# Cross attention's first half: heads 0 to 2 in an order written by hand, with the first two query products between the last output tiles

## The chip, the cores and the metric

The kernel runs on one core of a Trainium2 chip. The metric is the device time of one execution in microseconds (us); lower is better. The names of the engines are those of the profile: PE is TensorE's matrix multiply and PEld its weight load, DVE is VectorE, ACT is ScalarE, POOL is GpSimd, and SP is the engine whose queue issues the DMAs.

## What is computed

The reference is one decoder layer on 1024 tokens of width 1024, in float32. Only the middle of it is touched: the output product of the mixer adds to x, x is normalized by rows, and four cross-attention heads of width 256 read 256 memory tokens.

```python
x = x + jnp.concatenate([ml_out, fx_out], axis=-1) @ w_out[l]
x = x + cross_attention(rmsnorm(x, ln_x[l]), rmsnorm(mem, ln_mem[l]), w_xq[l], w_xkv[l], w_xo[l])
...
def cross_attention(h, memn, w_q, w_kv, w_o):
    q = (h @ w_q).reshape(B, S, X_HEADS, X_DH)
    ...
    s = jnp.einsum('bqhd,bmhd->bhqm', q, k) * (X_DH ** -0.5)
    p = jax.nn.softmax(s, axis=-1)
    o = jnp.einsum('bhqm,bmhd->bqhd', p, v).reshape(B, S, D)
    return o @ w_o
```

## The kernel before

Activations lie with features on the 128 partitions and tokens along the free axis. Every float32 product is made of three matmuls: each operand is cut into a rounded part (`hi`, copied by ACT, line 134 or 137) and the rest (`lo`, subtracted by DVE, line 135 or 138), and `mm3` (lines 186 to 188) adds lo by hi, hi by lo and hi by hi. The weight's lo part comes first, so a product can't start before DVE has cut its weights.

The tokens are worked in two halves of 512 (`hf` 0 and 1). The stage around the change runs so:

- Output tiles. There are 16 of them, 8 row blocks `n` in each half: nine matmuls of 128x512 each, in the order hf 0 with n 0 to 3, hf 1 with n 0 to 3, then the same with n 4 to 7. `full_sink` adds the residual that was loaded from `x1d` (DVE, line 1126), stores the sum, cuts it into `h2` for the first half (lines 137 and 138), and sums squares into `x1_accs[hf]`: the square is ACT's (line 222), the addition POOL's (line 226).
- `row_second(hf)` turns those sums into 1/rms. Four products with a column of ones (PE, line 234), then `rsqrt_cols`: DVE line 198, POOL line 204 (a power), DVE lines 206 to 208, which write `rcol`. For the second half `to_row` follows: PE transposes `rcol` (line 249), ACT copies it (line 250), and SP stores it to `rowd` and loads it back, spread over the partitions, as `row` (lines 251 and 253).
- The first half of each head `hd`. `query_whole` makes the two query products (24 matmuls of 128x512 each, into the banks `mm` and `m2`; the listings and the trace write `m` for `m2`) and cuts each into hi and lo. `right_side(hd)` prepares the second half's operands: two loads from `x1d`, a scaling by ACT (line 1177), seven cuts and four subtractions by POOL (line 1339), of which one feeds the next. `cross_head` loads the head's keys and values (lines 1276 and 1277), makes 24 score matmuls of 128x256, takes row maxima (DVE, lines 1289 and 1291), exponentials (ACT, line 1293), reciprocals (DVE, line 1294), scales the probabilities (ACT, line 1296), transposes them on PE (line 1301), and makes the two value products (12 matmuls of 128x512) into the single bank `ov`.
- The second half's heads follow, by blocks, with queries made in `query_blocks` from operands that `left_query` prepares.

Nothing in this stage has a fixed order before the change: the scheduler places each engine's instructions by its own model of time, subject to their dependencies. `in_order` is a helper that the first and the last stage use. Within it every compute engine (PE, ACT, DVE, POOL) keeps the order in which the code is written; SP's queue is still placed by the scheduler. Once compiled, either kernel has one fixed list of instructions for each engine, and an instruction that waits holds up all that stand behind it on its engine.

## Time and profile before

| what | value |
|---|---|
| median of the three runs | 1512.61 us |
| lowest and highest run | 1509.36 and 1513.43 us |
| profiled execution: span from first to last instruction, the only time that the page gives for it | 1509.2 us |
| PE busy | 1493.0 us, 99% of the span |
| PE weight loads busy | 1263.7 us, 84% |
| DVE / ACT / POOL busy | 1122.7 / 757.7 / 528.7 us |
| stage at hand: last output tiles, first half of the heads | about 592 to 705 us |

Times in the profile count from the span's start. A timeline row gives the start, the duration, the engine, the line, the operation and its output and inputs, and in brackets the idle time ahead of it with what ended it. Matmuls are pipelined: a 128x512 matmul is shown with about 0.39 us, but the next one starts 0.23 us after it. PEclk is the share of full clock that TensorE was granted.

### The profile page before, as it was taken

The numbers are of one execution on the slowest core, as the hardware profiler recorded it, in microseconds if no ns is written. First come the engines' busy times: TensorE is split into PE (matmuls) and PEld (weight loads), VectorE is DVE, ScalarE is ACT, GpSimd is POOL, SyncE is SP. The second block draws the span as 40 slices with busy tenths as digits, with TensorE's granted clock in tenths as the row PEclk, the third lists the DMA queues.
The fourth block names the chain that finished last, engine by engine and source line by source line (L and its number), as shares of the span: only waits on it lengthen the run. The fifth ranks groups of instructions, "written<-read, shape, count | busy, mean of one in ns | idle before, by whom it ended". The sixth has DMA issues, their size and how long they took to land.

```text
span 1509.2 us, 22358 instructions
## 1 busy us (share of the span) xinstructions
PE 1493.0 (99%) x7806; PEld 1263.7 (84%) x7806; DVE 1122.7 (74%) x1803; ACT 757.7 (50%) x1440; POOL 528.7 (35%) x545
## 2 busy tenths in 40 slices
PE   9999999999999999999999999999999999999997
PEld 9988888889899888788988878888888888888887
DVE  7766676664788875667767899989996678787765
ACT  7324343334688764566654467566664521122134
POOL 1003030414365441623300044454544365553312
PEclk9999999999999999999999999999999999999999
DMA  6322333435777877853354447676678677776623
GB/s 243 115 79 95 98 108 126 132 129 153 247 261 256 284 248 246 271 169 126 128 182 159 147 155 279 235 261 248 217 273 292 264 279 279 279 272 251 247 88 112
DMA packets 124276, 303.04 MB, mean 201 GB/s; under 512 B 13810, under 2 KB 28460, under 8 KB 117252
## 3 DMA queue, kind: packets, MB, share of 16 engines
q1 hardware_dynamic: 124164, 301.62, 57.3%
q8 instruction: 61, 1.00, 0.3%
q14 instruction: 51, 0.42, 0.1%
HBM read 202.75 MB, written 98.82 MB: 200 GB/s over the span
## 4 chain that ended last, share of the span: by engine, by line
PE 90%; DMA 4%; DVE 3%; ACT 1%; issue 1%; POOL 1%; POOLq 0%; DVEq 0%; SPq 0%; ACTq 0%
PE tp L186 8%; PE tp L187 8%; PE tp L188 8%; PE sc L186 6%; PE sc L188 6%; PE sc L187 6%; PE mm L186 5%; PE m L188 5%; PE m L186 5%; PE m L187 5%; PE mm L188 5%; PE mm L187 5%; PE ov L801 2%; PE ov L186 2%; PE ov L187 2%; PE ov L188 2%
## 5 line engine op out<-in xcount | busy, mean ns | idle before, releaser
L186 PE MATMUL tp<-act,wl 128*128 128x512 f32 (+1 forms) x440 | 172.6, 392 | 0.0
L187 PE MATMUL tp<-act,wh 128*128 128x512 f32 (+1 forms) x440 | 172.1, 391 | 0.0
L188 PE MATMUL tp<-act,wh 128*128 128x512 f32 (+1 forms) x440 | 171.8, 392 | 0.0
L135 DVE TENSOR_TENSOR wl<-wr,wh 128x1024 fp32r<-128x1024 f32 (+2 forms) x99 | 131.4, 1327 | 27.0 <-ACT wh L134 26.7
L134 ACT ACTIVATE wh<-wr 128x1024 fp32r<-128x1024 f32 (+2 forms) x99 | 99.8, 1008 | 85.7 <-PE tp L188 32.7
L186 PE MATMUL mm<-act,wl 128*128 128x512 f32 (+1 forms) x332 | 124.8, 376 | 2.6 <-DVE r_c L138 2.1
L188 PE MATMUL mm<-act,wh 128*128 128x512 f32 (+1 forms) x332 | 124.1, 374 | 0.0
L187 PE MATMUL mm<-act,wh 128*128 128x512 f32 (+1 forms) x332 | 123.8, 373 | 0.0
L186 PE MATMUL m<-act,wl 128*128 128x512 f32 (+1 forms) x308 | 113.8, 369 | 0.6 <-DVE wl L135 0.6
L188 PE MATMUL m<-act,wh 128*128 128x512 f32 (+1 forms) x308 | 113.8, 369 | 0.0
L187 PE MATMUL m<-act,wh 128*128 128x512 f32 (+1 forms) x308 | 113.7, 369 | 0.0
L188 PE MATMUL sc<-act,wh 128*128 128x512 f32 (+1 forms) x280 | 105.6, 377 | 0.0
L187 PE MATMUL sc<-act,wh 128*128 128x512 f32 (+1 forms) x280 | 105.6, 377 | 0.0
L186 PE MATMUL sc<-act,wl 128*128 128x512 f32 (+1 forms) x280 | 105.6, 377 | 0.0
L1612 POOL TENSOR_TENSOR z<-wr 128x256 f32<-128x256 f32 x56 | 52.9, 966 | 131.8 <-DMA wr<-w_ff2q 126.7
L188 PEld LDWEIGHTS tp<-act,wh 128*128 128x128 f32 x440 | 82.7, 188 | 19.0
L186 PEld LDWEIGHTS tp<-act,wl 128*128 128x128 f32 x440 | 82.7, 188 | 18.5
L187 PEld LDWEIGHTS tp<-act,wh 128*128 128x128 f32 x440 | 82.7, 188 | 18.2
L134 ACT ACTIVATE wh<-z 128x1024 fp32r<-128x1024 f32 (+1 forms) x54 | 55.5, 1027 | 81.8 <-POOL z L1612 62.3
L135 DVE TENSOR_TENSOR wl<-z,wh 128x1024 fp32r<-128x1024 f32 (+1 forms) x54 | 77.7, 1439 | 11.4 <-ACT wh L134 11.4
L134 ACT ACTIVATE w<-wr 128x768 fp32r<-128x768 f32 (+3 forms) x35 | 28.0, 801 | 107.4 <-PE tp L186 33.0
L186 PEld LDWEIGHTS mm<-act,wl 128*128 128x128 f32 x332 | 62.7, 189 | 14.2 <-DVE r_c L138 2.6
(734 smaller groups left out, 4387.2 us busy)
## 6 DMA issues: line engine op xcount, KB each, us to landing
act<-right SPq DMA_DIRECT2D x49, 1024.0 KB
right<-w SPq DMA_DIRECT2D x56, 256.0 KB
wr<-w_ff2q SPq DMA_DIRECT2D x28, 512.0 KB
right<-r_d SPq DMA_DIRECT2D x49, 256.0 KB
right<-r_e SPq DMA_DIRECT2D x49, 256.0 KB
act<-fqk SPq DMA_DIRECT2D x48, 256.0 KB
wr<-w_in SPq DMA_DIRECT2D x20, 512.0 KB
wr<-w_ff SPq DMA_DIRECT2D x20, 512.0 KB
```

What stands on the lines that cost most here:

```text
L134: s.activation(hi, src, AF.Copy)
L135: return v.tensor_tensor(out=lo, in0=src, in1=hi.bitcast(F32), op=ALU.subtract)
L186: nc.tensor.matmul(ps, w[1], x[0], start=first, stop=False, skip_group_check=more)
L187: nc.tensor.matmul(ps, w[0], x[1], start=False, stop=False, skip_group_check=more)
L188: nc.tensor.matmul(ps, w[0], x[0], start=False, stop=last, skip_group_check=more)
L801: nc.tensor.matmul(self.ov[:, c0:], self.fv[:, self.j], t[:, c0:], start=self.j == 0 and t is self.p[1], stop=self.last and t is self.p[0])
L1612: g.tensor_tensor(out=o, in0=x, in1=y, op=op)
```

## The change

The 16 output tiles become a generator, of which 14 run as before. Then, inside `in_order`, come the sums of `row_second(0)`, the first query product, the tile n = 6 of hf 1, the second query product and the tile n = 7. Heads 0 to 2 follow in written order: scores, the next head's first query product, transposes, the next head's second query product, values. `row_second(1)` and `to_row` stand inside head 0. For these three heads GpSimd scales the probabilities, and the second value product goes to a `tp` bank. Head 3 and all that follows stay with the scheduler.

```diff
     def row_second(hf):
         rsqrt_sums(x1_accs[hf], rcol[:, 4 * hf : 4 * hf + 4], 4)
-        if hf:
-            to_row(row, rcol, 8, rowd[2:3])
...
+    full = full_tiles()
+    for _ in range(14):
+        next(full)
...
+    def query_weights(n):
+        if n < KT:
+            w_query[n] = weights(a["w_xq"][n])
+
+    def query_product(n):
+        if n < KT:
+            ((_, _, p_query[n]),) = proj(w_query.pop(n), [h2], 1, order=[(0, 0)], into=ps_tile(("mm", "m2")[n % 2]))
+
+    def query_cut(n):
+        if n < KT:
+            queries[n] = q_room(n % 2)
+            split(*queries[n], p_query.pop(n), 1.0 / 16.0)
...
         for i in range(4):
-            s.activation(pr[:, i], pr[:, i], AF.Copy, scale=rden[:, i : i + 1])
+            if hf == 0 and hd < XH - 1:
+                g.tensor_scalar(out=pr[:, i], in0=pr[:, i], scalar1=rden[:, i : i + 1], scalar2=1.0, op0=ALU.mult, op1=ALU.mult)
+            else:
+                s.activation(pr[:, i], pr[:, i], AF.Copy, scale=rden[:, i : i + 1])
...
-            ov = ov_()
+            ov = tp() if kk and hf == 0 else ov_()
...
+    banks[:] = ["tp"]
+    row_second(0)
+    with in_order():
+        for n in range(2):
+            query_weights(n)
+        query_product(0)
+        next(full)
+        query_cut(0)
+        query_product(1)
+        next(full)
+        query_cut(1)
+        query_weights(2)
+        for hd in range(XH - 1):
+            steps = cross_head(hd, 0, [queries.pop(2 * hd + kk) for kk in range(2)], *os_[0])
+            next(steps)
+            query_product(2 * hd + 2)
+            if hd == 0:
+                row_second(1)
+            query_weights(2 * hd + 3)
+            side = right_steps(hd)
+            next(side)
+            next(steps)
+            query_cut(2 * hd + 2)
+            query_product(2 * hd + 3)
+            if hd == 0:
+                to_row(row, rcol, 8, rowd[2:3])
+            next(side, None)
+            query_weights(2 * hd + 4)
+            query_cut(2 * hd + 3)
+            for _ in steps:
+                pass
+    banks[:] = ["mm", "tp", "m2", "tp"]
+    right_side(XH - 1)
...
```

`right_steps` is `right_side` as a generator: its first step loads and scales and makes the three plain cuts, its second makes the subtractions and the cuts of their results.

What the compiled lists of instructions make of this is shown at three places. A name ends in the buffer's number; "waits" names the engines or DMA queues whose semaphores the instruction waits for.

First place, PE between the last output tiles and the first query product. Before: `tp_7092` is the last tile (hf 1, n 7), the line 234 products sum `r_b_6786`, which is `x1_accs[0]`, and `mm_7130` is the first query.

```order
L186 MATMUL tp_7092<-w_1275_6767,wl_6949 128x512
L187 MATMUL tp_7092<-w_1275_6767,wh_6948 128x512
L188 MATMUL tp_7092<-w_1275_6767,wh_6948 128x512
L234 MATMUL ov_7079<-ones,r_b_6786 128x1 [waits PE_49,Pool_49]
L234 MATMUL ov_7079<-ones,r_b_6786 128x1 x3
L186 MATMUL mm_7130<-act_6784,wl_7127 128x512 [waits DVE_49]
```

After, at the same place; `tp_7045` is the tile n 5 of hf 1, two tiles earlier, and `mm_7100` the first query:

```order
L187 MATMUL tp_7045<-w_1275_6767,wh_6942 128x512
L188 MATMUL tp_7045<-w_1275_6767,wh_6942 128x512
L234 MATMUL ov_7075<-ones,r_b_6786 128x1 [waits PE_49,Pool_49]
L234 MATMUL ov_7075<-ones,r_b_6786 128x1 x3
L186 MATMUL mm_7100<-act_6784,wl_7091 128x512 [waits DVE_49]
```

The sums of the first half stand two output tiles earlier on PE; the tiles n 6 and n 7 now come behind the first and the second query product. SP's list is the same in both kernels up to and with the stores of the tiles n 4 and n 5 of hf 1.

Second place, ACT at the end of the output tiles. Before: `r_c_7106` is the square of the last tile, `r_b_7122` and `r_p_7157` the hi cuts of the first and second query; the others belong to `right_side(0)` and to weights.

```order
L222 ACTIVATE r_c_7106<-r_p_7102 128x512 [waits DVE_49,Pool_49]
L134 ACTIVATE act_7192<-r_f_7197 128x256 [waits Activation_49]
L134 ACTIVATE act_7194<-r_f_7197 128x256
L134 ACTIVATE act_7193<-r_f_7196 128x256 [waits Pool_49]
L134 ACTIVATE act_7194<-r_f_7196 128x256 [waits Pool_49]
L137 ACTIVATE r_b_7122<-mm_7130 128x512 [waits PE_49]
L134 ACTIVATE wh_7358<-wr_7356 128x1024 [waits DMAHW6_49]
L134 ACTIVATE act_7193<-r_f_7196 128x256 [waits Pool_49]
L137 ACTIVATE r_p_7157<-m_1357_7165 128x512 [waits DMAHW7_49,DMAHW2_49,PE_49]
```

After; `r_c_7139` and `r_c_7185` are the squares of the tiles n 6 and n 7:

```order
L222 ACTIVATE r_c_7139<-r_e_7135 128x512 [waits DVE_49,Pool_49]
L137 ACTIVATE r_b_7142<-mm_7100 128x512 [waits PE_49]
L222 ACTIVATE r_c_7185<-r_p_7181 128x512 [waits DVE_49,Pool_49]
L137 ACTIVATE r_p_7188<-m_1352_7146 128x512 [waits DMAHW4_49,DMAHW7_49,DMAHW2_49,PE_49]
L134 ACTIVATE wh_7194<-wr_7192 128x1024
```

The last tile's square now stands directly ahead of the second query's cut, and the work of `right_side(0)` behind the exponentials. On DVE the last tile's addition likewise stands directly ahead of the second query's lo cut.

Third place, `row_second(1)` and `to_row`. Before, on DVE, they stood among head 2's row maxima; `c_var`, `c_t` and the last `rcol` row are `row_second(1)`, and `wl_7787` is a weight for the second half of the tokens:

```order
L198 TENSOR_SCALAR c_var_7306<-ov_7301 128x4 [waits PE_49]
L1289 TENSOR_REDUCE c_mx_7597<-sc_7599 128x2 [waits PE_49]
L1291 TENSOR_TENSOR c_mx_7597<-c_mx_7597,rcol 128x2 [waits DVE_49]
L206 TENSOR_TENSOR c_t_7310<-c_y_7308 128x4 [waits Pool_49]
L207 SCALAR_TENSOR_TENSOR c_t_7310<-c_t_7310,c_var_7306 128x4 [waits DVE_49]
L1294 RECIPROCAL c_rden_7596<-c_den_7595 128x4 [waits Activation_49]
L208 SCALAR_TENSOR_TENSOR rcol<-c_t_7310,c_y_7308 128x4 [waits DVE_49]
L138 SCALAR_TENSOR_TENSOR r_c_7670<-mm_7677,r_b_7669 128x512 [waits Activation_49]
L135 TENSOR_TENSOR wl_7787<-wr_7770,wh_7786 128x1024 [waits PE_49,Activation_49]
```

After, on DVE, in head 0; `wl_7290` is the lo cut of the weights for the product that stands on PE directly behind the transposes:

```order
L1306 RECIPROCAL c_rden_7208<-c_den_7207 128x4 [waits Activation_49]
L198 TENSOR_SCALAR c_var_7279<-ov_7274 128x4 [waits PE_49]
L206 TENSOR_TENSOR c_t_7283<-c_y_7281 128x4 [waits Pool_49]
L207 SCALAR_TENSOR_TENSOR c_t_7283<-c_t_7283,c_var_7279 128x4 [waits DVE_49]
L208 SCALAR_TENSOR_TENSOR rcol<-c_t_7283,c_y_7281 128x4 [waits DVE_49]
L135 TENSOR_TENSOR wl_7290<-wr_7287,wh_7289 128x1024 [waits DMAHW7_49,Activation_49]
```

Before, on ACT, around the copy of `row`; only work for the second half of the tokens and a value cut follow it:

```order
L134 ACTIVATE wh_7879<-wr_7772 128x1024 [waits Pool_49]
L250 ACTIVATE row<-ov_7314 8x128 [waits PE_49]
L1253 ACTIVATE r_f_7878<-mm_7883 128x256 [waits PE_49]
L134 ACTIVATE act_7120<-ov_7476 128x512 [waits PE_49]
L134 ACTIVATE w_1494_7915<-wr_7911 128x512 [waits DMAHW4_49,DMAHW3_49,PE_49]
```

After, on ACT, in head 0; `r_b_7323` and `r_p_7373` are the hi cuts of head 1's queries, and `act_7294`, `act_7295` the cuts of `right_steps`:

```order
L137 ACTIVATE r_b_7323<-mm_7249 128x512
L250 ACTIVATE row<-ov_7352 8x128 [waits PE_49]
L134 ACTIVATE act_7294<-r_f_7297 128x256 [waits Pool_49] x2
L134 ACTIVATE act_7295<-r_f_7297 128x256 [waits Pool_49]
L134 ACTIVATE wh_7369<-wr_7367 128x1024 [waits DMAHW3_49]
L137 ACTIVATE r_p_7373<-m_1391_7327 128x512 [waits DMAHW2_49]
```

Both have moved from the end of the first half into head 0, and what stands behind them on DVE and ACT is now what head 0's and head 1's next products on PE take. On PE the line 234 products of `row_second(1)` stand behind a whole query product (head 1's first) and the transpose of `rcol` (line 249) behind the next one (head 1's second). On SP the store and the load of `row` now stand ahead of the load of head 1's keys.

## The prediction

> **What bounds the kernel now.** I read the page, then the waits of PE in the stage at hand, then the granted clock there.

> ```profile
> PE 1493.0 (99%) x7806; PEld 1263.7 (84%) x7806; DVE 1122.7 (74%) x1803; ACT 757.7 (50%) x1440; POOL 528.7 (35%) x545
> PE 90%; DMA 4%; DVE 3%; ACT 1%; issue 1%; POOL 1%; POOLq 0%; DVEq 0%; SPq 0%; ACTq 0%
> PE mm L186 <- DVE r_c L138: 2.1, 1, 2.1
> ```

> PE is busy for 99% of the span and holds 90% of the chain that ended last, so a time that PE waits is added to the span. The third line is the whole answer on PE's waits between 592 and 700 us: one wait, before the first scores. It cost more than it shows:

> ```profile
> 639.20 0.39 PE L188 MATMUL m<-act,wh 128*128 128x512 f32 x1
> 641.74 0.50 PE L186 MATMUL mm<-act,wl 128*128 128x512 f32 x1 [2.14 <-DVE r_c L138]
> 639.05:642.46 3.41, 1.27 (x6) 0.74 (x5) 3.01 (x5) 2.86 (x7) 2.18 (x3) 1.00 0.64 252
> 642.46:645.88 3.42, 3.42 (x11) 2.65 (x10) 2.59 (x4) 2.10 (x4) 0.00 (x0) 0.50 0.87 287
> 1495.80:1499.20 3.40, 2.91 (x26) 2.71 (x24) 2.61 (x6) 2.04 (x6) 1.84 (x3) 1.00 0.46 157
> 1499.20:1502.60 3.40, 1.68 (x12) 1.40 (x12) 1.13 (x6) 0.78 (x2) 0.71 (x1) 1.00 0.44 152
> 1502.60:1506.00 3.40, 0.08 (x1) 0.00 (x0) 2.48 (x4) 0.00 (x0) 0.00 (x0) 0.50 0.47 159
> ```

> The first number after a stretch is its length, the next PE's busy time, and the last but two the granted clock. The stretch in which PE was busy for 1.27 of 3.41 us was followed by one of 3.42 us at clock 0.50; 1.68 of 3.40 near the end did the same, 2.91 of 3.40 did not. At half clock 3.42 us do the work of 1.71. So the one wait cost 2.1 + 1.7 = 3.8 us. This is all that the change can win in a stage without other waits: 0.25% of 1512.6.

> [...]

> **The change part by part.** The count of matmuls stays. What matters is where PE finds its next input late. Instructions that move are counted by what stands ahead of them on their engine now.

> (a) The sums of `row_second(0)` stand behind the tile n 5 of hf 1, two tiles earlier.

> ```profile
> 616.42 0.80 SPq L1125 DMA_DIRECT2D r_d<-x1d  x2
> 621.69 0.69 DVE L1126 TENSOR_TENSOR r_d<-m,r_d 128x512 f32<-128x512 f32 x1 [2.95 <-DMA r_d<-x1d]
> 623.80 3.00 POOL L226 TENSOR_TENSOR r_b<-r_c,r_b 128x512 f32<-128x512 f32 x2 [2.56 <-ACT r_c L222]
> 622.92 0.39 PE L188 MATMUL tp<-w,wh 128*128 128x512 f32 x1
> 627.35 0.95 PE L234 MATMUL ov<-ones,r_b 128*128 128x1 f32 x8
> 628.16 0.48 PE L186 MATMUL mm<-act,wl 128*128 128x512 f32 x1
> ```

> The residual of hf 0, n 6, lands for the addition at 621.69, though it was issued at 616.42. The squares of n 6 and n 7 are therefore added by POOL until 623.80 + 3.00 = 626.80. Before, line 234 came to PE at 627.35 and found the sum ready. Now PE is there at 622.92 + 0.23 = 623.15 and waits until 626.85: **3.7 us**. SP's, ACT's, DVE's and POOL's lists up to there are unchanged, so nothing comes sooner, and on PE both query products and two tiles are queued behind. The bounds: if the load lands without its 2.95 us of waiting, the sum is done about 3 us sooner and 0.7 is left; upwards I allow 0.5 us more, since PE's way to this point is the same.

> (b) Tile n 7 now lies between the second query product and the scores, as its cover. But ACT and DVE treat tile n 7 before they cut that query. From the tile's last matmul to the scores: DVE's addition, ACT's square, ACT's hi cut, DVE's lo cut.

> ```profile
> 631.07 0.68 DVE L1126 TENSOR_TENSOR r_p<-tp,r_p 128x512 f32<-128x512 f32 x1
> 627.16 0.61 ACT L222 ACTIVATE r_c<-r_d 128x512 f32<-128x512 f32 x1
> 641.93 0.59 ACT L137 ACTIVATE r_p<-m 128x512 fp32r<-128x512 f32 x1
> 641.01 0.68 DVE L138 SCALAR_TENSOR_TENSOR r_c<-mm,r_b 128x512 fp32r<-128x512 f32 x1
> ```

> 0.68 + 0.61 + 0.59 + 0.68 = 2.56, with handovers of about 0.05 each (641.01 + 0.68 to PE's 641.74) and 0.16 of drain 2.9; less ACT's overlap of the two (0.1), and three scores of 0.12 that need only the first query: **2.4 us**. So the old 2.14 us wait is not removed, only made by another chain. Bounds 2.0 and 2.9.

> (c) Head 0. Its third query product (head 1's first, 5.6 us) covers the softmax, see (e). Behind it come line 234 for `row_second(1)`, 8 transposes, and the next product, whose lo weights DVE cuts only after `rcol`.

> ```profile
> 679.27 1.03 PE L1301 MATMUL tp<-ident,z 128*128 128x128 f32 x8
> 631.67 0.15 DVE L198 TENSOR_SCALAR c_var<-ov 128x4 f32<-128x4 f32 x1
> 686.92 1.03 POOL L204 TENSOR_TENSOR c_y<-c_var,half 128x4 f32<-128x4 f32 x1
> 687.98 1.26 DVE L206 TENSOR_TENSOR c_t<-c_y 128x4 f32<-128x4 f32 x1 [1.01 <-POOL c_y L204]
> 689.28 0.16 DVE L207 SCALAR_TENSOR_TENSOR c_t<-c_t,c_var 128x4 f32<-128x4 f32 x1
> 690.16 1.22 DVE L135 TENSOR_TENSOR wl<-wr,wh 128x1024 fp32r<-128x1024 f32 x1
> ```

> From line 234's start: 0.95 + 0.15 + 1.03 + three small steps of 0.16 to 0.2 (0.6) + 1.22 + handovers (0.16) = 4.1 us. PE has 0.81 (627.35 to 628.16) and 0.87 of transposes (the row's 1.03 less a last drain) to do: it waits **2.4 us**. Nothing makes this shorter; if line 206 takes the 1.26 that it took beside POOL's work, 3.5.

> (d) Head 1's scores wait for its second query, which ACT cuts behind the copy of `row`, which waits for the transpose of `rcol` behind that same query product. From its end: line 250, cut t1, POOL's second and third subtraction, cut t3, weights, DVE's lo weights, DVE's lo cut.

> ```profile
> 693.85 0.25 ACT L250 ACTIVATE row<-ov 8x128 f32<-8x128 f32 x1
> L134 ACT ACTIVATE act<-r_f 128x256 fp32r<-128x256 f32 x24 | 9.1, 413 | 4.8 <-POOL r_f L1339 4.6
> L135 DVE TENSOR_TENSOR act<-r_f,act 128x256 fp32r<-128x256 f32 x24 | 12.2, 528 | 10.8 <-ACT act L134 10.5
> L1339 POOL TENSOR_TENSOR r_f<-r_f,r_f 128x256 f32<-128x256 f32 x8 | 6.5, 812 | 9.2 <-DVE act L135 4.7 <-ACT r_f L1177 4.2
> L134 ACT ACTIVATE wh<-wr 128x1024 fp32r<-128x1024 f32 x15 | 15.9, 1057 | 2.3 <-DMA wr<-w_xq 1.2 <-POOL wr L1227 1.1
> 696.76 0.33 SPq L251 DMA_DIRECT2D rowd<-row  x1
> 700.30 0.32 SPq L253 DMA_DIRECT2D row<-rowd  x1
> 642.11 0.38 SPq L1276 DMA_DIRECT2D w<-kxd  x1
> 645.59 0.41 PE L186 MATMUL sc<-w,r_c 128*128 128x256 f32 x1
> ```

> 0.25 + 0.41 + 0.53 + 0.81 + 0.81 + 0.41 + 1.06 + 1.22 + 0.68 = 6.2, with handovers 6.6 us. PE has 12 value matmuls of 0.233 and three scores of 0.12: 3.15. It waits 3.4 us at least. SP may add to it: the store of `row` waits for the same copy, its load for the store (3.5 us, 696.76 to 700.30), and only then go head 1's keys, which in head 0 landed within 3.5 us (642.11 to 645.59). That would be 0.4 + 3.5 + 0.4 + 3.5 = 7.8 us after the product, a wait of 5.0. The store took its 3.5 us in a busier stretch, so I stay between: **4.2 us**.

> (e) Scaling by GpSimd, 4 x 0.53 instead of ACT's 4 x 0.51:

> ```profile
> L767 POOL TENSOR_SCALAR w<-w,c_den 128x256 f32<-128x256 f32 x8 | 4.2, 528 | 2.1 <-DVE c_den L764 1.5 <-ACT r_a L137 0.5
> L1296 ACT ACTIVATE z<-z,c_rden 128x256 f32<-128x256 f32 x16 | 6.8, 509 | 0.0
> L1293 ACT ACTIVATE z<-sc,c_mx,rcol 128x256 f32<-128x256 f32 x16 | 8.8, 559 | 4.1 <-DVE c_var L198 3.3 <-DVE c_mx L1291 0.8
> 685.71 0.68 DVE L1289 TENSOR_REDUCE c_mx<-sc 128x2 f32<-128x512 f32 x1
> ```

> After the last score: maximum and product 0.9, two exponentials 1.3, reciprocal 0.2, POOL 2.1, handovers 0.3: 4.8 us, beside a query product of 24 x 0.233 = 5.6. Covered by 0.8; if POOL took twice as long, PE would wait 1.3 in each head. The second value bank costs nothing and, as PE never waited for `ov`, saves nothing. In heads 1 and 2 the second query's cut ends some 8.3 us after the transposes, against 5.6 + 2.8 + 0.35 of PE's work: covered by under half a microsecond, so I count **0.5 us** for both, bounds 0 and 4 (head 2 has the weights of the second half among its cuts).

> Sum of waits: 3.7 + 2.4 + 2.4 + 4.2 + 0.5 = 13.2. Each of the first four is as long as the one that halved the clock, but a gap may fall across two stretches, and then neither need be idle enough: I count three falls of four, 5.1 us. Less the old 3.8: **+14.5 us**. The span was 1509.2, near the lowest run, 1509.36; on the median of 1512.6 it makes 1527.1.

> **Rivals.**
> - The written order is covered, not slower: at each place what PE needs is ready. Then only the old wait goes: 1512.6 - 3.8 = 1508.8. It decides at (d): the chain of 6.6 us must end within PE's 3.15. For it speaks that (e) fits; against it, that three chains hang on PE's own position and can't run ahead.
> - The late load of (a) was an accident of this execution and SP's part of (d) is hidden: 0.7 + 2.4 + 2.4 + 3.4 + 0.5, two clock falls of 1.7, less 3.8: +9.0, 1521.6.
> [...]
> - More waits in heads 1 and 2 and where head 3 meets the second half's operands, whose cuts stand ahead of head 2's exponentials on ACT and wait for a DMA: up to 4 more, the fourth clock fall and one more (3.4): +21.9, 1534.5.

> **How the numbers follow.** Forecast 0.42, around 1527; early load 0.20; clock only after long gaps 0.12; more waits 0.11; covered 0.08; and 0.07 for a part of the waits only, 1511 to 1516. Leaving out the last two, the range is 1516 to 1537: the lower end takes every wait at its lower bound with one clock fall (0.7 + 2.0 + 2.4 + 3.4 + 1.7 - 3.8 = +6.4, and a run 3 us under the median), the upper the last rival with 2 us for the spread of the runs (1509.36 to 1513.43). A difference within 0.3% (4.5 us) can't be told from none. Covered is within it, but for a spread in its favour (0.04 faster); of the partial case about half is the same: faster 0.04, same 0.08, slower 0.88.

> **What would show it.** Right: PE waits of line 234 for POOL's `r_b` near 623 us (3.7), of the first scores for DVE's `r_a` (2.3), of `m` line 186 for `wl` (2.4) directly behind head 0's transposes, of head 1's scores for `r_y` or the keys' DMA (3.4 to 5), each with clock 0.5 soon behind it. No wait for POOL at the transposes. Wrong: PE without waits from 623 to 700 us, or line 234 finding its sum ready.

## The result and the profile after

| what | before | after |
|---|---|---|
| median (lowest to highest), four runs each | 1511.67 us (1509.36 to 1513.43) | 1538.22 us (1536.42 to 1541.62) |
| span of the profiled execution | 1509.2 us | 1539.9 us |
| ratio after to before | | 1.018, 95% interval 1.0167 to 1.0192 |

The change costs 26.5 us. The forecast had said slower, by 14.5; 1538.2 lies 1.2 us above its range. The profiled execution is the slowest of the four (1541.62 us for a span of 1539.9), so the two spans differ by 30.7. The mean granted clock was 0.990 in it and 0.991 in the other three, which fits one or two slow stretches fewer there (an estimate from these means).

On the page, PE's busy time has grown by 10.8 us with the same 7806 matmuls, which is a slower clock (granted 0.990 in the mean, 0.997 before); the rest of the 30.7 is waiting:

```profile
PE 1503.8 (98%) x7806; PEld 1272.1 (83%) x7806; DVE 1125.2 (73%) x1803; ACT 753.7 (49%) x1428; POOL 534.8 (35%) x557
```

PE's waits between 600 and 770 us, where before there was one of 2.1 and one of 0.4:

```profile
PE sc L186 <- DMA w<-kxd: 4.2, 1, 4.2
PE sc L186 <- DVE r_y L138: 3.5, 2, 2.5
PE ov L234 <- POOL r_b L226: 3.4, 1, 3.4
PE sc L186 <- DVE r_a L138: 2.4, 1, 2.4
PE m L186 <- DVE wl L135: 2.2, 1, 2.2
PE mm L186 <- ACT r_f L1265: 2.0, 1, 2.0
PE sc L186 <- ACT act L134: 1.1, 1, 1.1
PE m L187 <- DVE act L135: 1.0, 1, 1.0
PE tp L1316 <- POOL z L1309: 0.8, 2, 0.5
PE sc L187 <- DVE act L135: 0.5, 1, 0.5
PE ov L186 <- ACT row L250: 0.4, 1, 0.4
```

The numbers are the sum, the count and the longest. Together 21.5 us. The rows with `r_b`, `r_a`, `wl`, `row` and `kxd` are the four foreseen places, 12.6 us. The transposes and head 3's scores (`r_y`, once 2.5) make 3.3. What is left, 5.6 us, lies behind head 3's scores, at the first products of the second half's queries (`r_f`, `act`) and at its first scores (`r_y`, once 1.1).

The clock, by stretches (length, PE's busy time, ..., granted clock third from the end):

```profile
625.25:628.66 3.41, 1.01 (x9) 1.01 (x10) 3.41 (x4) 2.49 (x4) 2.78 (x3) 1.00 0.69 228
628.66:632.07 3.41, 3.41 (x10) 2.67 (x10) 1.36 (x3) 0.00 (x0) 3.41 (x3) 0.50 0.98 314
673.03:676.45 3.42, 0.13 (x1) 0.00 (x0) 3.15 (x5) 2.13 (x4) 0.16 (x1) 1.00 0.98 293
676.45:679.86 3.41, 2.51 (x12) 2.54 (x13) 0.31 (x1) 0.00 (x0) 0.00 (x0) 0.50 1.02 404
679.86:683.27 3.41, 3.41 (x16) 3.31 (x16) 1.28 (x3) 1.20 (x4) 0.00 (x0) 0.50 0.83 333
717.41:720.82 3.41, 1.53 (x14) 1.33 (x12) 3.41 (x4) 1.76 (x5) 2.96 (x3) 1.00 0.63 182
720.82:724.23 3.41, 2.84 (x24) 2.84 (x25) 3.41 (x6) 3.17 (x7) 1.81 (x2) 1.00 0.32 123
```

There are five falls: near 629, 649 and 663 for one stretch each, near 676 and 731 for two each. That is 23.9 us at half clock, with PE busy for 22.0 of it, so 11.0 lost by the granted clock of 0.50, and 1.7 before. Both are estimates: from 629.05 to 631.62 the 128x512 matmuls start 0.43 us apart, for 0.23 at full clock, and by these starts the 11.0 would be 10.0. The rows from 673 show a double fall: PE enters the first slow stretch still waiting for the keys, is busy in 2.51 of it, and the next is slow too.

Waits 21.5 - 2.5 and clock 11.0 - 1.7 give 28.3 of the 30.7 us. By the n-th matmul of either trace PE was 0.9 us behind before the stage began, 6 at the first scores, 9 in head 0, 22 in head 2, 30.6 at the second half's first queries, and 30.5 at the end: nothing is won back later.

### The profile page after: what moved, and what is told of

Its sections match the earlier page's. It is cut to its first block, busy times and chain, and to the rows that moved or that the text cites. A ratio compares the mean times of both kernels' runs of the same rounds, so it can differ in the third digit from the quotient of the medians.

```text
span 1539.9 us, 22376 instructions
## 1 busy us (share of the span) xinstructions
PE 1503.8 (98%) x7806; PEld 1272.1 (83%) x7806; DVE 1125.2 (73%) x1803; ACT 753.7 (49%) x1428; POOL 534.8 (35%) x557
## 4 chain that ended last, share of the span: by engine, by line
PE 89%; DMA 4%; DVE 3%; ACT 1%; POOL 1%; issue 1%; SPq 0%; POOLq 0%; DVEq 0%; ACTq 0%
PE tp L186 8%; PE tp L187 8%; PE tp L188 8%; PE sc L186 6%; PE sc L188 6%; PE sc L187 6%; PE mm L186 5%; PE m L186 5%; PE m L188 5%; PE mm L187 5%; PE mm L188 5%; PE m L187 5%; PE ov L801 2%; PE ov L186 2%; PE ov L187 2%; PE ov L188 2%
## 5 line engine op out<-in xcount | busy, mean ns | idle before, releaser
L186 PE MATMUL tp<-act,wl 128*128 128x512 f32 (+1 forms) x442 | 173.4, 392 | 0.0
L188 PE MATMUL tp<-act,wh 128*128 128x512 f32 (+1 forms) x442 | 172.6, 392 | 0.0
L135 DVE TENSOR_TENSOR wl<-wr,wh 128x1024 fp32r<-128x1024 f32 (+2 forms) x99 | 132.0, 1334 | 26.5 <-ACT wh L134 25.8
L134 ACT ACTIVATE wh<-wr 128x1024 fp32r<-128x1024 f32 (+2 forms) x99 | 99.7, 1007 | 88.6 <-PE tp L188 36.3
L186 PE MATMUL mm<-act,wl 128*128 128x512 f32 (+1 forms) x332 | 125.3, 377 | 2.0 <-ACT r_f L1265 2.0
L188 PE MATMUL mm<-act,wh 128*128 128x512 f32 (+1 forms) x332 | 124.5, 375 | 0.0
L186 PE MATMUL m<-act,wl 128*128 128x512 f32 (+1 forms) x306 | 114.5, 374 | 2.8 <-DVE wl L135 2.8
L188 PE MATMUL m<-act,wh 128*128 128x512 f32 (+1 forms) x306 | 114.1, 373 | 0.0
L186 PE MATMUL sc<-act,wl 128*128 128x512 f32 (+1 forms) x280 | 106.0, 378 | 1.1 <-ACT act L134 1.1
L188 PE MATMUL sc<-act,wh 128*128 128x512 f32 (+1 forms) x280 | 105.6, 377 | 0.0
L188 PEld LDWEIGHTS tp<-act,wh 128*128 128x128 f32 x442 | 83.1, 188 | 19.0
L186 PEld LDWEIGHTS tp<-act,wl 128*128 128x128 f32 x442 | 83.1, 188 | 18.6
L134 ACT ACTIVATE wh<-z 128x1024 fp32r<-128x1024 f32 (+1 forms) x54 | 55.5, 1027 | 79.0 <-POOL z L1655 59.5
L135 DVE TENSOR_TENSOR wl<-z,wh 128x1024 fp32r<-128x1024 f32 (+1 forms) x54 | 77.1, 1427 | 7.4 <-ACT wh L134 7.4
L134 ACT ACTIVATE w<-wr 128x768 fp32r<-128x768 f32 (+3 forms) x35 | 28.0, 800 | 107.0 <-PE tp L186 33.0
L186 PEld LDWEIGHTS mm<-act,wl 128*128 128x128 f32 x332 | 63.5, 191 | 13.4 <-ACT r_f L1265 2.2
```

The lines of the kernel that those rows point to most:

```text
L134: s.activation(hi, src, AF.Copy)
L135: return v.tensor_tensor(out=lo, in0=src, in1=hi.bitcast(F32), op=ALU.subtract)
L186: nc.tensor.matmul(ps, w[1], x[0], start=first, stop=False, skip_group_check=more)
L188: nc.tensor.matmul(ps, w[0], x[0], start=False, stop=last, skip_group_check=more)
```

## The experiments

Each kernel is the changed one with one edit, unless said otherwise. In brackets stands the 95% interval of the ratio to the kernel before, which took 1511.1 to 1512.3 us beside them.

**1. The sums of the first half later.**

```diff
-    row_second(0)
     with in_order():
...
         query_product(1)
+        row_second(0)
         next(full)
```

> The changed kernel with one edit: the sums of row_second(0) stand behind the second query product instead of ahead of the first. Its PE wait for POOL there was 3.45 us (before 627.65), and the clock was halved for one full stretch of 3.41 us behind it, in which PE was busy throughout. Theory A (each wait on PE adds its own length and the clock fall that follows): both go, 3.45 + 1.7 = 5.2 us less than the changed kernel; since DVE now makes rcol just ahead of the last tile's addition, up to 0.7 of it comes back at the first scores: 4.5 to 5.2. Rival B (the later waits only grow by what this one gave the other engines in time): 0 to 2 us less, with the waits of the first scores or of head 0's second product longer than 2.4 and 2.2.

1540.9 us [1.0167 to 1.0204]: nothing won, nearer to the rival than to theory A. (In the changed kernel the call stands just ahead of `in_order`, not inside it; the compiled list has the sums ahead of the first query product all the same.) PE's rows with a wait there, ahead of the first query product and of the first scores:

```profile
625.11 0.50 PE L186 MATMUL mm<-act,wl 128*128 128x512 f32 x1 [1.82 <-DVE r_p L1126]
646.82 0.58 PE L186 MATMUL sc<-w,r_a 128*128 128x256 f32 x1 [3.28 <-DVE r_a L138]
```

Line 234 no longer waits, but the query product waits for line 1126: the bank `mm` is held by an output tile whose addition stands on DVE behind one that waits for its residual (2.22 us, DVE's wait for `r_d<-x1d`). The chain behind the late load is the same, whoever meets it first.

**2. The second query's cut ahead of the last tile's sink.** The generator yields once more between the last tile's matmuls and its `full_sink`.

```diff
                     for k in range(3):
                         mm3(ps, ...)
+                    if hf and n == 7:
+                        yield
                     full_sink(n, hf, ps)
...
         query_cut(1)
+        next(full)
```

> The changed kernel with one edit: the last output tile's matmuls stay where they are, but its addition, store and square are written behind the cut of the second query instead of ahead of it. Theory A: the wait of the first scores (2.36 us) goes, since ACT's and DVE's cut take 1.5 us beside a tile of 2.1 us, and with it the halved clock of 649.1 to 652.6 (3.41 us busy, 1.7 us): 4.1 us less. Rival B: the last tile's work, now behind the cut, delays the weights of the next product or the row maxima, and half or more of it comes back in head 0: 0 to 2 us less.

1538.5 us [1.0147 to 1.0194]. The 2.36 us before the first scores went; 1.1 of it came back at the next query product, whose weights ACT and DVE now cut behind the last tile's sink (`wl`, 650.73 for 648.67). The rest was taken by the clock, which fell for two stretches at line 234 here (628.42 to 635.25, behind a wait of 3.70 us), and once more at 720.58, behind a stretch with PE busy for 1.48 us.

**3. The second query's weights ahead of `row_second(1)`.**

```diff
             query_product(2 * hd + 2)
+            query_weights(2 * hd + 3)
             if hd == 0:
                 row_second(1)
-            query_weights(2 * hd + 3)
```

> The changed kernel with one edit: the weights of the product behind the transposes are cut ahead of row_second(1) on ACT and DVE instead of behind it. Theory A: the wait for wl directly behind head 0's transposes (2.16 us) goes with its clock fall (3.42 us at half clock, 1.7 us): 3.9 us less. Rival B: row_second(1) now delays to_row and with it head 1's scores by as much: about 0.

1537.0 us [1.0147 to 1.0177]. The wait for `wl` is gone. The profiled span is 4.7 us shorter, the median only 1.3, within what these runs scatter; a wait of 2.14 us at 755, 1.07 in the changed kernel, halved the clock anew, with PE busy for 1.27 us of the stretch that it fell in.

**4. The row's transpose, copy, store and load behind the heads.**

```diff
-            if hd == 0:
-                to_row(row, rcol, 8, rowd[2:3])
...
+    to_row(row, rcol, 8, rowd[2:3])
     banks[:] = ["mm", "tp", "m2", "tp"]
```

> The changed kernel with one edit: to_row stands behind the three heads instead of in head 0. Theory A (to_row alone holds head 1's scores, by SP's queue and by ACT's): the waits for the row copy (0.36) and for the keys' DMA (4.19) go with two stretches of halved clock (5.9 us busy, 3.0): 7.5 us less. Rival B (the cuts of right_steps hold the query's cut also without the row copy): the scores wait for DVE's r_y instead, 1.5 to 3 us, and only 3 to 5 us are won.

1531.7 us [1.0105 to 1.0141], 6.5 less: the waits for `row` and the keys are gone, and between head 0's second product and head 3's scores PE waits for nothing longer than 0.55 us. This is the dearest single place of the change.

**5. All four edits.**

> All four single edits together: the sums of the first half behind the last output tile and both first query products' place kept, the second query's cut ahead of the last tile's residual and square, the weights of head 1's second query ahead of the second half's sums, and the copy of the row behind the heads. Theory A (each wait is made at its own place and they add up): the waits of 3.45, 2.36, 2.16 and 4.55 us go, with the half clock behind them (four of five falls, about 8 us): 1538 - 12.5 - 8 = about 1518; the waits at head 3 (2.5) and at the second half's first operands (4.7) stay, with one fall. Theory B (what is taken away at one place comes back at the next, since PE runs ahead of the cuts): new waits of 1 to 4 us in place of those removed, 1528 to 1533, no better than the row's edit alone (1531.7).

1527.1 us [1.0087 to 1.0127]. PE's waits from 600 to 705 us:

```profile
PE mm L186 <- DVE r_p L1126: 3.8, 1, 3.8
PE sc L186 <- DVE r_a L138: 1.3, 1, 1.3
PE mm L186 <- DVE wl L135: 1.0, 1, 1.0
PE tp L1318 <- POOL z L1311: 0.9, 2, 0.5
PE sc L186 <- DVE r_y L138: 0.7, 1, 0.7
```

Just under theory B's range. Of the 12.5 us of waits at the four places 6.8 are left, half of it behind the late residual; head 3's 2.1 and the 4.5 behind it stayed.

**6. ACT scales heads 0 to 2 again.**

```diff
-            if hf == 0 and hd < XH - 1:
+            if hf > 1:
                 g.tensor_scalar(out=pr[:, i], ...)
             else:
                 s.activation(pr[:, i], pr[:, i], AF.Copy, scale=rden[:, i : i + 1])
```

`hf` is 0 or 1, so the branch of ACT is always taken.

> ACT scales the probabilities of heads 0 to 2 again, all else as changed. Theory A (the waits at head 3 and at the second half's operands come from GpSimd's scaling: 3.2 us for four in heads 1 and 2, with GpSimd's subtractions and so the last operands behind it): the transposes' waits (0.8), the wait before head 3's scores (2.45) and those at 726 to 732 us (4.7) shrink to 3 us or less together, and a fall of the clock goes with them: 1530 to 1533. Theory B (they come from the written place of the right side's work, behind two weights and a query cut): the transposes still do not wait, but the wait before head 3's scores and at 726 to 732 us stays at 6 to 8 us: 1536 to 1540.

1543.8 us [1.0193 to 1.0227], slower by 5.6 than with GpSimd. Both theories missed this:

```profile
707.28 1.71 ACT L1311 ACTIVATE z<-z,c_rden 128x256 f32<-128x256 f32 x4 [0.24 <-DVE c_rden L1306]
708.89 1.04 ACT L134 ACTIVATE wh<-wr 128x1024 fp32r<-128x1024 f32 x1
```

On ACT the scaling stands ahead of the cut of the weights for the product behind head 2's transposes, and that product waits 1.4 us for `wl`, as it did not before; the operands behind head 3's scores come later still. GpSimd's scaling relieves the written order; it does not cause the waits near head 3.

**7. The change without the written order.**

```diff
-    with in_order():
+    if True:
```

> The change without the written order: same parts in the same code, but the scheduler places heads 0 to 2 and the last two output tiles by its own model. Theory A (the written order is what costs; scaling by GpSimd and the second value bank cost nothing): the scheduler interleaves scores with the next query product, so PE always has something, 1509 to 1514 us, as before the change. Theory B (the parts cost too: sums early, GpSimd's scaling of 0.8 us each beside DVE): 1518 to 1526.

1515.4 us [1.0017 to 1.0038], 4.0 above the kernel before and between the theories. So 22.8 of the 26.5 us are the written order's. What is left is mostly the sums two tiles early and the row's transpose:

```profile
PE ov L249 <- DVE rcol L208: 1.4, 1, 1.4
PE ov L234 <- POOL r_b L226: 1.4, 1, 1.4
```

**8. Head 2 left to the scheduler.** The loop's body runs inside `in_order` for heads 0 and 1 and outside it for head 2.

> The written order holds for the last tiles and heads 0 and 1 only; head 2 is placed by the scheduler together with head 3. Theory A (the waits at head 3 and the second half's operands, 7 to 8 us and one double stretch at half clock, are made by head 2's written order): they go, the four earlier waits stay as they are: 1538 - 7.5 - 3.4 = 1527. Theory B (they come from the delay that heads 0 and 1 have built up on ACT and DVE): they stay within 2 us: 1535 to 1540.

1537.55 us [1.0151 to 1.0182]. PE's waits from 700 to 770 us:

```profile
PE sc L186 <- DVE r_y L138: 2.3, 1, 2.3
PE sc L186 <- DVE r_f L1253: 1.1, 1, 1.1
PE m L186 <- DVE r_f L1253: 1.0, 1, 1.0
PE sc L186 <- DVE r_a L138: 0.6, 1, 0.6
PE tp L1316 <- POOL z L1309: 0.5, 1, 0.5
```

The 4.7 us from 726 to 732 are gone with their two slow stretches, though `r_f` now costs 2.1 further on. Between head 1 and the second half's first queries PE lost 7.5 us here and 14.2 in the changed kernel. The span is 3.0 us shorter, since some 2.5 were lost again behind that point, and the median only 0.7: the profiled execution of the changed kernel is 3.4 us above its median, this one 1.0. So theory A is right about the operands, and theory B about the time and head 3's scores.

**9. The four edits without the written order** (5 and 7 together).

> The four edits of place without the written order: the scheduler places the last tiles and heads 0 to 2, and the sums of the first half, the weights and the row's copy stand later in its list. Theory A (what is left of 4 us in the version without the order is the sums two tiles early, 1.4 us of waiting and one fall of the clock, and the row's transpose in head 0, 1.4 us): both waits and the fall go, 1509 to 1511.5, at or just under the time before the change. Theory B (it is the scaling by GpSimd and the bank, or later queries of the second half): 1514 to 1517 as without the edits.

1512.0 us [0.9997 to 1.0015]: not to be told from the kernel before, and 3.4 less than 7. The waits that are left:

```profile
PE sc L186 <- DVE r_c L138: 1.3, 1, 1.3
PE tp L1318 <- POOL z L1311: 1.2, 2, 1.0
PE ov L234 <- POOL r_b L226: 1.0, 1, 1.0
```

The transpose's wait is gone, line 234's is not, and no stretch of the stage ran at half clock. With the four edits in both, the written order costs 15.1 us (1527.1 in 5).

**10. Head 1's keys ahead of the row.** Its loads are issued before `to_row`.

> Head 1's keys and values are loaded ahead of the store and the load of the row; ACT still copies the row ahead of the second query's cut. Theory A (the wait before head 1's scores has two chains, and ACT's and DVE's cut of the query was ready 1.8 us ahead of the keys): the keys' wait of 4.2 us goes and a wait for r_y of 2.2 to 2.6 us stands in its place, with at least one stretch at half clock: 1535 to 1537. Theory B (the keys alone): no wait over 1 us before head 1's scores, 1530 to 1532 as when the row is copied later.

1538.15 us [1.0161 to 1.0189], as changed. The two chains of the place are both real: the keys' 4.2 us went, and under it lay

```profile
PE sc L186 <- DVE r_y L138: 2.1, 1, 2.1
```

so ACT's copy of the row alone costs 2.1 + 0.4 us, and SP's queue adds 2. The span is 2.7 us shorter and the median the same: the slow stretch saved near 680 came back at 718.21, behind head 3's scores.

**11. The kernel before with two parts alone**: GpSimd's scaling in heads 0 to 2, and the second values in a `tp` bank.

> The kernel before with two parts of the change alone: GpSimd scales the probabilities of heads 0 to 2, and their second value product goes to a tp bank. Theory A (these two parts cost nothing where the scheduler places the work): 1510 to 1514, no new wait of over 0.5 us. Theory B (GpSimd's scaling takes 3.2 us for four beside DVE's cuts and makes the transposes wait): 1514 to 1518.

1512.9 us [0.9995 to 1.0017]: the same as before, theory A by the time. The scheduler's order moved with it; 0.8 us of waiting for POOL at one head's transposes is the longest that comes of it.

**12. The four edits, and head 2 free** (5 and 8 together).

> All four edits of place, and head 2 left to the scheduler: only the last tiles and heads 0 and 1 are in written order. Theory A (the causes add up): the 4.7 us of waits at the second half's first operands and the stretches at half clock behind them go, as with head 2 free alone: 1527 - 4.7 - 3 = about 1519. Theory B (the delay only moves): 1525 to 1529.

1522.1 us [1.0052 to 1.0083], 5.1 less than 5: between the theories. No stretch of the stage ran at half clock, although head 3's scores waited 2.38 us: by stretches counted on in steps of 3.41 us (an estimate, since no change of the clock marks their ends here) that gap fell across two, and PE was busy for 2.27 and 2.16 us of them:

```profile
700.66:704.08 3.42, 2.27 (x18) 1.90 (x16) 1.92 (x4) 3.42 (x9) 1.65 (x3) 1.00 0.28 111
704.08:707.49 3.41, 2.16 (x18) 2.16 (x19) 3.41 (x8) 1.71 (x5) 0.00 (x0) 1.00 0.03 5
```

**13. The fourth block's cuts behind head 2.** `right_side(3)` and the cuts of `t4` move into the written order, behind head 2's values.

> As changed, but the right side of head 3 and the cuts of the fourth block (line 135, act from w) stand in written order behind head 2's values, so on DVE they no longer stand ahead of the cut of head 2's second product (r_y). Theory A (three of those cuts, 4.4 us beside GpSimd's subtractions, make head 3's scores wait): the wait of 2.45 us before head 3's scores falls under 0.5 us; what PE waits for at the second half's first operands (4.7 us) stays or grows by up to 2: 1534 to 1539. Theory B (the product itself ends late and its cut takes its 1.3 us anyway): the wait of 2 to 2.5 us stays: 1537 to 1541.

1540.4 us [1.0178 to 1.0212]. Theory A by the wait, though not by its time of 1534 to 1539: the cut of `r_y` now starts at 715.54 instead of 720.66 and head 3's scores don't wait, but

```profile
PE mm L187 <- DVE act L135: 2.3, 1, 2.3
PE m L186 <- ACT act L134: 0.9, 1, 0.9
PE mm L186 <- ACT r_f L1265: 0.8, 1, 0.8
```

stand directly behind, and four stretches at half clock follow, from 725.36 to 739.01.

## Why the prediction was right in sign and short in size

(a) **Line 234**: 3.45 us, foreseen 3.7, by the chain named. The load was no accident of one execution, as a rival had it: line 234 waits 2.6 to 4.7 us in all eight kernels in written order that leave the sums there. Experiment 1 adds what the working did not say: moving the sums does not help, since the bank of the first query product hangs on the same load.

(b) **First scores**: 2.36, foreseen 2.4; experiment 2 shows the cause. The working put the old wait of 2.14 us before the first scores. Its row is `mm<-act`, head 1's first query product, which waited until the first query was cut out of the bank `mm`; the scheduler then set head 0's scores among that product's matmuls. The sum does not change by this.

(c) **The second product's weights**: 2.16, foreseen 2.4, by the chain named; in experiment 3 the wait is gone.

(d) **Head 1's scores**: 0.36 + 4.19, foreseen 4.2, but the path was the upper one of the two:

```profile
669.77 0.27 ACT L250 ACTIVATE row<-ov 8x128 f32<-8x128 f32 x1 [8.54 <-PE ov L249]
671.29 0.33 SPq L253 DMA_DIRECT2D row<-rowd  x1
671.67 0.42 SPq L1288 DMA_DIRECT2D w<-kxd  x1
674.89 0.68 DVE L138 SCALAR_TENSOR_TENSOR r_y<-m,r_p 128x512 fp32r<-128x512 f32 x1
677.35 0.55 PE L186 MATMUL sc<-w,r_c 128*128 128x256 f32 x1 [4.19 <-DMA w<-kxd]
```

`r_y` was ready at 675.57; the keys, issued at 671.67, set the end at 677.35. The store took 1.2 us and not 3.5 (670.06 to 671.29), the keys 5.7 and not 3.5, with the row's load in front of them and a DMA share of 0.98; how much of the 5.7 that load makes, no run separates. The two errors cancelled, which was luck. Experiment 10 took the one chain off the other.

(e) **"I count 0.5 us for both, bounds 0 and 4"** is the first step that failed. Heads 1 and 2 and what they hand on cost 9.0 us: 0.8 at the transposes, 2.45 at head 3's scores, 4.7 at the second half's operands, 1.1 at its first scores. The working let the cut of the second query end some 8.3 us after the transposes. From the end of the last transpose it took 7.2 us in head 1 (689.54 to 696.77) and 12.9 in head 2 (708.48 to 721.34). It was sized by each engine's mean durations, and beside another engine's work the same operations took longer here:

```profile
655.28 1.84 POOL L1309 TENSOR_SCALAR z<-z,c_rden 128x256 f32<-128x256 f32 x4 [6.72 <-DVE c_rden L1306]
704.43 3.22 POOL L1309 TENSOR_SCALAR z<-z,c_rden 128x256 f32<-128x256 f32 x4 [10.04 <-DVE c_rden L1306]
716.37 4.37 DVE L135 TENSOR_TENSOR act<-w,act 128x256 fp32r<-128x256 f32 x3
717.55 1.48 POOL L1355 TENSOR_TENSOR wr<-w,wr 128x512 f32<-128x512 f32 x1
720.66 0.68 DVE L138 SCALAR_TENSOR_TENSOR r_y<-m,r_p 128x512 fp32r<-128x512 f32 x1
```

Four scalings take 1.84 us in head 0, beside no work of DVE, and 3.22 in head 2, where DVE cuts weights from 705.10 to 706.44, and head 2's transposes wait 0.8 us for GpSimd, against the sign "No wait for POOL at the transposes". Three cuts by DVE, 0.53 each by the mean that the prediction used, take 4.37 beside three GpSimd operations, and the cut of head 2's last query product (`r_y`, for head 3's scores) stands behind them. The GpSimd operations beside them took 1.3 to 1.5 us, and each cut ended 0.28 to 0.29 us after the one beside it; the fourth cut of the block, at 729.53 with GpSimd idle until 0.3 us later, took 0.42. Why the cuts took longer there, no run shows. Experiment 13 shows that these cuts made head 3's scores wait, experiment 8 that head 2's written order made the operands late. For the 1.1 us at the second half's first scores no run shows the cause. The rival "more waits in heads 1 and 2 and where head 3 meets the second half's operands" was the case that came. It had a chance of 0.11, and 4 us more of waiting where 8.5 came. The wait for a DMA that it names was there (ACT stood idle for 2.03 us until 700.59, just ahead of head 2's exponentials), but the larger waits came behind the transposes.

**"I count three falls of four, 5.1 us"** is the second. The lost clock was 11.0 us. That a gap may fall across two stretches fits experiment 12 (2.38 us of waiting and no half clock, its stretches counted on by estimate), but here all four gaps halved the clock, and a fifth did at the second half's operands. One fall was priced at one stretch, 1.7 us; two of the five lasted two. What the chance of 0.12 stood for, a clock that falls only after long gaps, did not come: gaps of 2.36 and 2.16 us halved it near 649 and 663. So the terms of the sum are: waits (a) to (d) 12.5 where the prediction had 12.7, (e) 9.0 for 0.5, clock 11.0 for 5.1, less 4.2 for the old 3.8.

**Scaling and bank** cost nothing in the scheduler's order (experiment 11). In the written order the scaling costs the 0.8 us at head 2's transposes, and ACT's costs more (experiment 6).

What stays open: which gap halves the clock changes from kernel to kernel (2.38 us in experiment 12 did not, 2.14 us in experiment 3 did), so the medians of single edits carry some us that belong to no edit; and 2.4 us of the 30.7, of which 0.9 was there before the stage began. No version here beats the kernel before.

## What to carry to other kernels

Here an order written by hand for all engines tied each engine's queue to the slowest chain in it: a row's transpose, copy, store and load, needed only by the second half and written ahead of heads 1 and 2 instead of behind them, cost 6.5 us, and the scheduler's own order of the same work cost 23 us less than the written one. Ahead of such a change, follow each queue past the edited part to where its work is handed on, and price operations by rows in which the engines are busy together as they will be (three DVE cuts beside GpSimd took 4.37 us, for 1.6 by their mean; four scalings beside DVE 3.22, for 1.84). Mend it as a whole: three of the four single edits won at most 1.3 us, since waits came back or the clock fell at other places, and only the edits and the free order together gave all of the time back.

## What the runs showed of the hardware

```profile
717.17:720.58 3.41, 1.48 (x13) 1.28 (x12) 3.41 (x4) 2.11 (x5) 2.78 (x2) 1.00 0.63 203
720.58:723.99 3.41, 3.03 (x14) 3.03 (x15) 3.41 (x6) 2.80 (x7) 1.79 (x2) 0.50 0.24 90
```

(These two are of experiment 2; the row of 1.53 is shown with the result.) At half clock (0.50), after up to 2.88 us of PE busy (experiment 13) the slow clock stayed, after 2.90 (experiment 3) and more it ended, but for three of line 234's stretches (3.01 to 3.06 in experiments 2, 8 and 13). Taken at 0.50, an estimate, 2.88 and 2.90 us are 1.44 and 1.45 us of work at full clock, near the 1.48. The 1.60 and the 1.68 fell although 1.53 and 1.55 did not: why is open.
